# Other orders for the weight sums, the weight forms and the late activation forms of a two-layer transformer's feed-forward blocks

## The chip, the cores and the metric

The kernel runs on one NeuronCore of a Trainium2 chip. The core has a matrix engine (TensorE, PE in the profile, with its weight loads listed apart as PEld), a vector engine (VectorE, DVE), an activation engine (ScalarE, ACT), a general engine (GpSimd, POOL) and a queue engine (SyncE, SP) that issues transfers. The metric is the device time of one execution in microseconds; of several runs the median is taken. Lower is better.

## The reference

A sequence of 512 rows of width 1024 goes through two layers. Each layer has an attention part, which the change does not touch, and a feed-forward part with a squared ReLU:

```python
for l in range(DEPTH):
    ...
    x = x + jnp.einsum('bse,ed->bsd', mixed, w_o[l])

    h = rmsnorm(x, mlp_norm[l])
    u = jnp.square(jax.nn.relu(jnp.einsum('bsd,df->bsf', h, w_ff1[l])))
    x = x + jnp.einsum('bsf,fd->bsd', u, w_ff2[l])
return rmsnorm(x, final_norm)
```

`w_ff1` is 1024 by 4096 and `w_ff2` is 4096 by 1024, both float32.

## The kernel before

**Precision.** Every float32 operand of a product is split into two parts: `hi`, a rounded copy made by ACT (line 114 for weights, 236 or 241 for activations), and `lo`, the rest, made by DVE (line 130, 237 or 242). Three matmuls then stand for one product (`three`, lines 296 to 298). So each block of weights ("unit") costs one ACT instruction `whi` and one DVE instruction `wlo` over 128x1024 elements before PE can use it. Four pairs of buffers hold split weights in the feed-forward part; a unit is split when the unit four places before it has left PE, three units ahead of its use.

**Seven products for eight.** The feed-forward width is cut into 4 groups. In each group both products are done as a 2x2 block product with seven block multiplications in place of eight (Strassen's scheme in Winograd's form). The seven forms are named by their weight operand: `11`, `21` and `22` are quadrants as they lie in memory, `x1` to `x4` are sums of quadrants. The weight sums chain: `x3` = 12 + 22, `x2` = 11 + x3, `x1` = 12 + 11, `x4` = 21 + x2, up to signs. `FORMS` (line 41) is the order in which the seven are multiplied.

**The first product** (`quad_group`, from line 1006; groups 1 to 3, two halves j = 0 and 1 each; units `("s", l, g, j, form)`). Five places in SBUF hold its raw weights, called by letters: a, b, c are buffers of their own (`first_a`, `first_b`, `first_c` in the trace), d is `waves` and e is `norms`. A place serves the forms in `serves` (line 869). `bring` loads a place from memory; e takes two transfers, a load from SP's queue and then an accumulating transfer from POOL's queue that adds the second quadrant, the second waiting for the first. `add` (line 887) sums one place into another on DVE, 128x1024 elements. When each of these is traced is fixed by `then(unit, fn, ...)`: it is traced right after the split of that unit (lines 902 to 914). Results lie in PSUM banks X, V and Y; after form `x1` DVE reads X (line 1036), and form `22` writes into X again, with form `x4` between them in V.

**The second product** (loop from line 1184; units `("f", l, g, form, c)`, c = 0 and 1, 12 matmuls over 512 columns each). Its raw weights live in three kept places, `HOME` (line 43). The sums are made by accumulating transfers in POOL's queue (`grow`, line 857): after the split of `11` its place gets 12 added and becomes `x1`; after `x3` its place gets 11 and becomes `x2`; after `x2` it gets 21 and becomes `x4`; after `21` the place is loaded with 22. Products of `11`, `x2`, `x1` and `22` accumulate on the same two PSUM banks X (`CHAIN`, line 44), `x3` (and in the last group `x4`) on V, `21` on Y, `x4` of the other groups on fresh banks W. After a form whose sum belongs to an output quadrant (`SUMS`, line 45) `gather` (line 1071) reads the two banks into `y`, on DVE (line 1079) or, for a quadrant's first contribution in layer 0, on ACT (line 1077). A form that goes on in X must wait until these reads are done.

**The activation's forms.** The activations of the second product have seven forms too, `sides[j]`. Four are made inside `quad_group`; three late ones (operands for `x2`, `21`, `22`) are made by `rest_of_forms` (line 1053) for both j, the first after both halves and the others after the forms `11`, `x3` and `x2` of the second product.

**What sets the order on an engine.** The program is traced in the order of the code, and a scheduler then orders the instructions of each engine: what was traced first goes first among those that it takes to be ready. Each engine's order is fixed before the run; on the chip every engine works through its queue in that order, and an instruction that waits holds up all behind it on its engine.

Of the kernel before, what the change touches and what calls it, by code (L numbers as in the profile page):

```python
# [13 lines left out]
ALU = mybir.AluOpType  # L14
# [24 lines left out]
DLY_R, DLY_D, DLY_S, DLY_Q = 3.5, 10.2, 9.0, 6.0  # L39
TAIL, ATT, DENSE, CAP = 6.0, 53.0, 145.0, 0.1  # L40
FORMS = ("11", "x3", "x2", "21", "x1", "x4", "22")
SIDE = {"11": 0, "x4": 1, "21": 2, "x1": 3, "x3": 4, "x2": 5, "22": 6}
HOME = {"11": 0, "x1": 0, "x3": 1, "x2": 1, "x4": 1, "22": 2, "21": 2}
CHAIN = {"11": "X", "x2": "X", "x1": "X", "22": "X", "x3": "V", "x4": "V", "21": "Y"}
# [5 lines left out]
def _unit_list():  # L50
    units = []
    def qk(l, cq, ck, b):
        units.append(("p", l, cq + b * P))
        units.append(("p", l, ck + b * P))

    for l in range(L):
        for item in ORDER:
            b = int(item[1])
            if item[0] == "d":
                units.append(("x", l, b, 0))  # L60
                units.append(("x", l, b, 1))
            elif item[0] == "s":
                qk(l, SBQ, SBK, b)
            else:
                for half in range(2):
                    units.append(("v", l, (SBV if item[0] == "u" else DFV) + b * P, half))
        for half in (1, 0):
            for j in range(4):
                units.append(("o", l, half, j))
        for g in range(GROUPS):  # L70
            if g == 0:
                units.extend(("1", l, f) for f in range(2 * GP))
            else:
                units.extend(("s", l, g, j, form) for j in range(2) for form in FORMS)
            for form in FORMS:
                for c in range(GP // 2):
                    units.append(("f", l, g, form, c))
    return units
# [84 lines left out]
def trunk(ctx, tc, opened, xT, w, w2, w1, gfin, lamv, cos, sin, out):  # L163
# [76 lines left out]
    def split_less(hi, lo, src):  # L240
        a = nc.scalar.activation(hi, src, AF.Copy, scale=-1.0)
        nc.vector.scalar_tensor_tensor(
            out=lo, in0=src, scalar=-1.0, in1=hi.bitcast(F32), op0=ALU.mult, op1=ALU.subtract)
        return a
# [87 lines left out]
    for l in range(L):  # L332
        with ExitStack() as actx:
# [476 lines left out]
            for cost in dense(pts if l else None):  # L810
# [5 lines left out]
                while live and credit > 0:  # L816
                    c = next(at, None)
# [17 lines left out]
        with ExitStack() as fctx:  # L835
# [28 lines left out]
            def then(unit, fn, *args):  # L864
                W.then.setdefault(_INDEX[unit], []).append(lambda: fn(*args))

            groups = [(g, j) for g in range(1, GROUPS) for j in range(2)]
            spots = {"d": kept[(2, 1)], "e": norms.rearrange("p a t -> p (a t)")}
            serves = {"a": ("11", "x2"), "b": ("x1",), "c": ("22",), "d": ("21", "x4"), "e": ("x3",)}

            def bring(n, role):
                if n == len(groups):
# [27 lines left out]
                then(("1", l, k), bring, 0, role)  # L900
            then(("f", l, 0, "x2", 1), bring, 0, "e")
            for n, (g, j) in enumerate(groups):
                then(("s", l, g, j, "11"), add, "b", "a")
                then(("s", l, g, j, "x3"), add, "a", "e")
                then(("s", l, g, j, "x3"), bring, n + 1, "e")
                then(("s", l, g, j, "21"), add, "d", "a")
                then(("s", l, g, j, "21"), bring, n + 1, "a")
                then(("s", l, g, j, "x1"), bring, n + 1, "b")
                then(("s", l, g, j, "22"), bring, n + 1, "c")
                if j == 0:  # L910
                    then(("f", l, g - 1, "22", 1), bring, n, "d")
                    then(("s", l, g, j, "x4"), bring, n + 1, "d")
                else:
                    then(("s", l, g, j, "x4"), fetch, g, "21", 1)
# [88 lines left out]
            def chunk(j, k):  # L1003
                return x[:, ((4, 5, 6, 7), (4, 5, 0, 1))[j][k], :]

            def quad_group(g, j, banks_):
# [8 lines left out]
                for form in FORMS:  # L1015
# [9 lines left out]
                    if form == "11":  # L1025
                        nc.scalar.copy(Y, X)
                    elif form == "x3":
                        nc.scalar.copy(v3, V)
                    elif form == "x2":
                        nc.scalar.copy(sx, X)  # L1030
                    elif form == "21":
                        nc.scalar.activation(F[1], Y, AF.Relu)
                        nc.scalar.activation(F[1], F[1], AF.Square)
                        split(hi[0], lo[0], F[1])
                    elif form == "x1":
                        nc.vector.scalar_tensor_tensor(  # L1036
                            out=F[2], in0=X, scalar=-1.0, in1=v3, op0=ALU.mult, op1=ALU.subtract)
                    elif form == "x4":
                        tt2(F[0], V, sx, ALU.add)
                        nc.scalar.activation(both, both, AF.Relu)  # L1040
                        nc.scalar.activation(both, both, AF.Square)
                        split(hi[1], lo[1], F[2])
                        tt2(F[1], F[1], F[0], ALU.subtract)
                        tt2(F[0], F[2], F[0], ALU.subtract)
                        tt2(F[2], F[2], F[1], ALU.add)
                        split(sides[j][0][:, 3:5, :, :].rearrange("p k a t -> p (k a t)"),
                              sides[j][1][:, 3:5, :, :].rearrange("p k a t -> p (k a t)"),
                              x[:, 4:6, :].rearrange("p c t -> p (c t)"))
                    else:
                        nc.scalar.activation(F[3], X, AF.Relu, scale=-1.0)  # L1050
                        nc.scalar.activation(F[3], F[3], AF.Square)

            def rest_of_forms(form):
                for j in range(2):
                    F = [chunk(j, k) for k in range(4)]
                    hi, lo = ([e[:, k, :, :].rearrange("p a t -> p (a t)") for k in range(7)] for e in sides[j])
                    if form == "":
                        split_less(hi[5], lo[5], F[2])
                    elif form == "11":
                        split(hi[2], lo[2], F[3])  # L1060
                    elif form == "x3":
                        tt2(F[3], F[2], F[3], ALU.subtract)
                    elif form == "x2":
                        split(hi[6], lo[6], F[3])

            fresh = set() if last else set(y)

# [95 lines left out]
            for g in range(GROUPS):  # L1163
                end = g == GROUPS - 1
                turn[0] = 0
                if g:
                    p_, q_, r_, s_ = r_, s_, p_, q_
                    quad_group(g, 0, (p_, q_, r_))
                    quad_group(g, 1, (s_, r_, q_))
                    rest_of_forms("")  # L1170
                else:
                    for k in range(2 * GP):
                        for n, pt in enumerate(block(f"f{l}_{g}_{k}", "any")):
# [7 lines left out]
                    p_, q_, r_, s_ = ring[0] % 3, 3, (ring[0] + 1) % 3, (ring[0] + 2) % 3  # L1181
                    held_on = {"Y": [bank("t", f"Y{l}{r}") for r in range(2)], "V": [bank("mm", f"V{l}{r}") for r in range(2)]}
                chains = {"X": [temp(k, f"X{l}{g}{k}") for k in (p_, q_)], **held_on}
                for form in FORMS:
                    total, to = SUMS[form], chains[CHAIN[form]]
                    opens = form == "11" or g == 0 and form in ("x3", "21")
                    if form == "x4" and not end:
# [42 lines left out]
                        break  # L1230
                    if end or form not in ("x3", "21"):
                        came = gather(total, to)
                    if g:
                        rest_of_forms(form)
                    if end and not last and form in ("x2", "21"):
                        for c in range(4 * (form == "21"), 4 * (form == "21") + 4):
                            nc.sync.dma_start(x[:, c, :], park[c])
                    if end and last and form == "x3":
                        for c in range(2):
# [105 lines left out]
```

## Time and profile before

| | |
|---|---|
| median of 3 runs | 1138.74 us (1137.9 to 1139.2) |
| the profiled execution | 1137.62 us |
| its span, first to last instruction | 1135.8 us |
| PE busy | 1120.2 us (99%) |
| DVE busy | 897.8 us (79%) |
| ACT busy | 686.8 us (60%) |
| POOL busy | 151.5 us (13%) |
| HBM read | 152.86 MB |

The profiled execution's own time is 1.8 us above its span, which is what lies around the program's instructions. The page's busy share of PE counts each matmul from its start to its modelled end; since matmuls overlap, the distance between starts tells more. In the timeline each row is one run of equal instructions: start, duration, engine, line, what it writes and reads, and in brackets the idle time of the engine before it and what ended it. In the rows of transfers the last number is the median time from issue to landing.

### The profile page before, as it was taken

The page shows a single profiled execution, that of the slowest core. Times are in us where ns is not written, and L with a number is a line of the kernel's source. Part 1 is how long each engine was busy: PE and PEld are TensorE (multiplying, and loading weights), DVE is VectorE, ACT ScalarE, POOL GpSimd, SP SyncE. Part 2 cuts the span into 40 slices and gives each one's busy share as a digit, 9 for nine tenths or more (in the row PEclk, how much of TensorE's full clock was granted, in tenths as well). Part 3 has the DMA queues.
Part 4 walks back from the last instruction along what each step waited for, and adds up shares of the span by engine and source line. Part 5 has one row for each costly group of instructions (what it writes and reads, how often), then busy time and mean ns, then how long its engine had stood idle before and what let it go on. Part 6 is the DMA issues. An engine that isn't in the chain of part 4 may idle for free.

```text
span 1135.8 us, 17692 instructions
## 1 busy us (share of the span) xinstructions
PE 1120.2 (99%) x6613; PEld 992.8 (87%) x6613; DVE 897.8 (79%) x1313; ACT 686.8 (60%) x1115; POOL 151.5 (13%) x237
## 2 busy tenths in 40 slices
PE   9999999999999999999999999999999999999997
PEld 7899889888889899898888998988888998988975
DVE  7897788789559778787888877887876787786876
ACT  6456666577558457466455565765773574764754
POOL 1000333101101101001000013330011010010010
PEclk9999999999999999999999999999999999999999
DMA  7665353266976857838327644522489679588282
GB/s 263 146 177 148 100 166 108 75 218 166 252 188 167 209 172 168 239 113 214 122 75 197 174 117 142 150 74 75 151 204 231 174 167 235 141 183 223 91 163 79
DMA packets 61621, 183.38 MB, mean 161 GB/s; under 512 B 7520, under 2 KB 8800, under 8 KB 61536
## 3 DMA queue, kind: packets, MB, share of 16 engines
q1 hardware_dynamic: 50160, 141.84, 39.4%
q0 software_dynamic: 10944, 39.85, 20.1%
q8 instruction: 52, 0.85, 0.3%
q10 hardware_dynamic: 432, 0.56, 0.1%
q14 instruction: 33, 0.27, 0.1%
HBM read 152.86 MB, written 4.19 MB: 138 GB/s over the span
## 4 chain that ended last, share of the span: by engine, by line
PE 82%; issue 8%; DMA 4%; DVE 3%; ACT 1%; POOL 1%; POOLq 0%; DVEq 0%; ACTq 0%
PE X L296 6%; PE X L297 6%; PE X L298 6%; PE wo L296 3%; PE wo L297 3%; PE wo L298 3%; PE f L298 3%; PE f L296 3%; PE f L297 3%; PE V L298 2%; PE V L297 2%; PE V L296 2%; DVE wlo L130 2%; PE Y L298 2%; PE Y L297 2%
## 5 line engine op out<-in xcount | busy, mean ns | idle before, releaser
L130 DVE TENSOR_TENSOR wlo<-q,whi 128x1024 fp32r<-128x1024 f32 x96 | 116.7, 1222 | 56.7 <-ACT whi L114 53.6
L114 ACT ACTIVATE whi<-q 128x1024 fp32r<-128x1024 f32 x96 | 100.8, 1056 | 91.7 <-DMA q<-in_w 28.0
L114 ACT ACTIVATE whi<-raw 128x1024 fp32r<-128x1024 f32 (+1 forms) x82 | 80.8, 993 | 50.4 <-issue 20.4
L130 DVE TENSOR_TENSOR wlo<-raw,whi 128x1024 fp32r<-128x1024 f32 (+1 forms) x82 | 95.2, 1168 | 12.1 <-ACT whi L114 11.6
L296 PE MATMUL X<-whi,Ah 128*128 128x512 f32 x248 | 97.8, 395 | 1.9 <-ACT whi L114 1.3
L297 PE MATMUL X<-wlo,Ah 128*128 128x512 f32 x248 | 97.4, 393 | 0.8 <-DVE wlo L130 0.8
L298 PE MATMUL X<-whi,Al 128*128 128x512 f32 x248 | 97.1, 391 | 0.0
L862 POOL DMA_DIRECT2D q<-in_w x48 | 42.4, 884 | 237.3 <-DVE wlo L130 223.9
L130 DVE TENSOR_TENSOR wlo<-waves,whi 128x1024 fp32r<-128x1024 f32 x40 | 48.9, 1222 | 17.1 <-ACT whi L114 17.1
L114 ACT ACTIVATE whi<-waves 128x1024 fp32r<-128x1024 f32 x40 | 42.3, 1057 | 32.7 <-PE X L298 16.6
L296 PE MATMUL X<-hxh,whi 128*128 128x256 f32 x192 | 54.6, 285 | 3.4 <-DVE x L1036 3.4
L296 PEld LDWEIGHTS X<-whi,Ah 128*128 128x128 f32 x248 | 46.9, 189 | 12.2 <-ACT whi L114 1.7
L297 PEld LDWEIGHTS X<-wlo,Ah 128*128 128x128 f32 x248 | 47.0, 190 | 10.4 <-DVE wlo L130 1.1
L298 PEld LDWEIGHTS X<-whi,Al 128*128 128x128 f32 x248 | 47.0, 189 | 9.9
L298 PE MATMUL X<-h_hi,wlo 128*128 128x256 f32 x192 | 54.3, 283 | 0.0
L297 PE MATMUL X<-h_lo,whi 128*128 128x256 f32 x192 | 54.3, 283 | 0.0
L298 PE MATMUL X<-hxh,wlo 128*128 128x256 f32 x192 | 54.3, 283 | 0.0
L297 PE MATMUL X<-hxl,whi 128*128 128x256 f32 x192 | 54.3, 283 | 0.0
L296 PE MATMUL X<-h_hi,whi 128*128 128x256 f32 x192 | 54.3, 283 | 0.0
L236 ACT ACTIVATE Ah<-x 128x512 fp32r<-128x512 f32 (+1 forms) x60 | 42.6, 710 | 16.5 <-DVE x L940 16.1
L296 PE MATMUL f<-h_hi,whi 128*128 128x512 f32 x128 | 50.3, 393 | 0.0
L298 PE MATMUL f<-h_hi,wlo 128*128 128x512 f32 x128 | 49.9, 390 | 0.0
(738 smaller groups left out, 3805.3 us busy)
## 6 DMA issues: line engine op xcount, KB each, us to landing
raw<-in_w SPq DMA_DIRECT2D x78, 512.0 KB, 3.7
q<-in_w POOLq DMA_DIRECT2D x64, 512.0 KB, 6.6
q<-in_w SPq DMA_DIRECT2D x48, 512.0 KB, 5.4
waves<-in_w SPq DMA_DIRECT2D x28, 512.0 KB, 5.5
first_a<-in_w SPq DMA_DIRECT2D x12, 512.0 KB, 3.8
first_b<-in_w SPq DMA_DIRECT2D x12, 512.0 KB, 4.8
first_c<-in_w SPq DMA_DIRECT2D x12, 512.0 KB, 3.5
norms<-in_w SPq DMA_DIRECT2D x12, 512.0 KB, 3.7
```

Of the source, the lines that this page charges most:

```text
L114: return self.nc.scalar.activation(o, src, AF.Copy)
L130: self.last = h, nc.vector.tensor_tensor(out=lo[:, a:b], in0=raw[:, a:b], in1=hi[:, a:b].bitcast(F32), op=ALU.subtract)
L236: a = nc.scalar.activation(hi, src, AF.Copy)
L296: nc.tensor.matmul(pt, ah, bh, start=first, stop=False, skip_group_check=goes_on)
L297: nc.tensor.matmul(pt, ah, bl, start=False, stop=False, skip_group_check=goes_on)
L298: nc.tensor.matmul(pt, al, bh, start=False, stop=last, skip_group_check=goes_on)
L862: nc.gpsimd.dma_start(t, quad(g, q, c), accum_op=ALU.add)
```

## The change

It has three parts.

1. **First product.** The place e now serves `x3` and `x2`, and a serves `11` alone: after the split of `x3`, a is added into e (before, e was added into a). The sum b += a is traced after the split of `21` in place of after that of `11`. The sum into d is taken from e. The next load of e is traced after the split of `21`, behind that of a, in place of after that of `x3`. The number of sums (3) and of transfers is the same.
2. **Second product.** A second order, `FORMS2`, is used for it: `21` comes third and `x2` fourth. So `x2` and `x1`, both on X, now stand side by side, and `x2` stands four units behind `x3` in place of two.
3. **Late activation forms.** `rest_of_forms` takes one j. For j = 0 the three are traced inside the second half of `quad_group` (after `11`, `x3`, `x2`), for j = 1 after both halves and after `11` and `x3` of the second product. The operand of `21` comes first, then that of `x2`, then that of `22`.

```diff
 FORMS = ("11", "x3", "x2", "21", "x1", "x4", "22")
+FORMS2 = ("11", "x3", "21", "x2", "x1", "x4", "22")
...
-            for form in FORMS:
+            for form in FORMS2:
                 for c in range(GP // 2):
                     units.append(("f", l, g, form, c))
...
-            serves = {"a": ("11", "x2"), "b": ("x1",), "c": ("22",), "d": ("21", "x4"), "e": ("x3",)}
+            serves = {"a": ("11",), "b": ("x1",), "c": ("22",), "d": ("21", "x4"), "e": ("x3", "x2")}
...
             for n, (g, j) in enumerate(groups):
-                then(("s", l, g, j, "11"), add, "b", "a")
-                then(("s", l, g, j, "x3"), add, "a", "e")
-                then(("s", l, g, j, "x3"), bring, n + 1, "e")
-                then(("s", l, g, j, "21"), add, "d", "a")
+                then(("s", l, g, j, "x3"), add, "e", "a")
+                then(("s", l, g, j, "21"), add, "b", "a")
+                then(("s", l, g, j, "21"), add, "d", "e")
                 then(("s", l, g, j, "21"), bring, n + 1, "a")
+                then(("s", l, g, j, "21"), bring, n + 1, "e")
                 then(("s", l, g, j, "x1"), bring, n + 1, "b")
                 then(("s", l, g, j, "22"), bring, n + 1, "c")
...
                     else:
                         nc.scalar.activation(F[3], X, AF.Relu, scale=-1.0)
                         nc.scalar.activation(F[3], F[3], AF.Square)
-
-            def rest_of_forms(form):
-                for j in range(2):
-                    F = [chunk(j, k) for k in range(4)]
-                    hi, lo = ([e[:, k, :, :].rearrange("p a t -> p (a t)") for k in range(7)] for e in sides[j])
-                    if form == "":
-                        split_less(hi[5], lo[5], F[2])
-                    elif form == "11":
-                        split(hi[2], lo[2], F[3])
-                    elif form == "x3":
-                        tt2(F[3], F[2], F[3], ALU.subtract)
-                    elif form == "x2":
-                        split(hi[6], lo[6], F[3])
+                    if j and form in ("11", "x3", "x2"):
+                        rest_of_forms(0, {"11": "21", "x3": "x2", "x2": "22"}[form])
+
+            def rest_of_forms(j, form):
+                F = [chunk(j, k) for k in range(4)]
+                hi, lo = ([e[:, k, :, :].rearrange("p a t -> p (a t)") for k in range(7)] for e in sides[j])
+                if form == "21":
+                    split(hi[2], lo[2], F[3])
+                elif form == "x2":
+                    split_less(hi[5], lo[5], F[2])
+                elif form == "22":
+                    tt2(F[3], F[2], F[3], ALU.subtract)
+                    split(hi[6], lo[6], F[3])
...
-                    rest_of_forms("")
+                    rest_of_forms(1, "21")
...
-                for form in FORMS:
+                for form in FORMS2:
...
-                    if g:
-                        rest_of_forms(form)
-                    if end and not last and form in ("x2", "21"):
-                        for c in range(4 * (form == "21"), 4 * (form == "21") + 4):
+                    if g and form in ("11", "x3"):
+                        rest_of_forms(1, "x2" if form == "11" else "22")
+                    if end and not last and form in ("21", "x2"):
+                        for c in range(4 * (form == "x2"), 4 * (form == "x2") + 4):
                             nc.sync.dma_start(x[:, c, :], park[c])
```

## The prediction

> **What bounds the kernel now.** I read the page first, then the waits of PE, then all waits, then timelines around each place where PE stood still.
>
> ```profile
> PE 1120.2 (99%) x6613; PEld 992.8 (87%) x6613; DVE 897.8 (79%) x1313; ACT 686.8 (60%) x1115; POOL 151.5 (13%) x237
> PE X L296 <- DVE x L1036: 3.4, 3, 2.4
> PE X L296 <- ACT whi L114: 1.3, 1, 1.3
> PE X L297 <- DVE wlo L130: 0.8, 1, 0.8
> PE X L296 <- DVE y L1079: 0.6, 1, 0.6
> ```
>
> PE is the bound, and its matmuls stay as they are. The rows of waits (total, times, longest) show all that PE loses in the feed-forward parts: 3.4 + 1.3 + 0.8 + 0.6 = 6.1 us in six stops. The change can gain these and what follows each, and no more; it can lose without such a limit.
>
> The 3.4 us: DVE reads X after form `x1` (line 1036), and `22` waits for that.
>
> ```profile
> 336.19 1.23 DVE L888 TENSOR_TENSOR first_b<-first_b,first_a 128x1024 f32<-128x1024 f32 x1 [5.62 <-DMA first_b<-in_w]
> 341.47 0.68 DVE L1036 SCALAR_TENSOR_TENSOR x<-X,x 128x512 f32<-128x512 f32 x1
> 339.41 0.28 PE L297 MATMUL V<-h_lo,whi 128*128 128x256 f32 x1
> 339.53 0.28 PE L298 MATMUL V<-h_hi,wlo 128*128 128x256 f32 x1
> 342.20 0.39 PE L296 MATMUL X<-hxh,whi 128*128 128x256 f32 x1 [2.40 <-DVE x L1036]
> DVE first_b L888 <- DMA first_b<-in_w: 20.7, 6, 5.6
> ```
>
> DVE stood 5.62 us at the sum b += a, whose b had not landed; everything behind it came late, line 1036 among it, and PE stopped 2.40 us. Six such stops of DVE make 20.7 us; three reached PE.
>
> The 1.3 and 0.8 us lie in the last group of layer 1, at `x2` of the second product:
>
> ```profile
> 1086.47 0.63 ACT L1243 ACTIVATE x<-x 128x512 f32<-128x512 f32 x1 [2.72 <-DMA x<-in_gfin]
> 1098.94 1.06 ACT L114 ACTIVATE whi<-q 128x1024 fp32r<-128x1024 f32 x1 [3.65 <-DMA q<-in_w]
> 1095.84 0.40 PE L296 MATMUL X<-whi,Ah 128*128 128x512 f32 x1
> 1100.05 0.51 PE L296 MATMUL X<-whi,Ah 128*128 128x512 f32 x1 [1.32 <-ACT whi L114]
> 1101.89 0.62 PE L296 MATMUL X<-whi,Ah 128*128 128x512 f32 x1
> 1102.31 0.63 PE L297 MATMUL X<-wlo,Ah 128*128 128x512 f32 x1
> 1105.53 0.39 PE L296 MATMUL Y<-whi,Ah 128*128 128x512 f32 x1
> 1101.90:1105.30 3.40, 3.40 (x10) 2.63 (x9) 3.40 (x5) 1.03 (x2) 0.59 (x1) 0.50 0.71 123
> ```
>
> ACT waited for the accumulated weights of the second `x2` unit. The form lasted from 1095.84 to 1105.53, 9.69 us, also because the clock was halved after the two stops: in the last row (a stretch, the busy time of PE, PEld, DVE, ACT and POOL in it, then granted clock, DMA share and GB/s) it is 0.50 over 3.40 us, and matmuls start 0.42 apart.
>
> The 0.6 us is `x2` waiting for DVE's reading of X after `11`, in the last group of layer 0.
>
> ```profile
> 532.86 0.39 PE L298 MATMUL V<-whi,Al 128*128 128x512 f32 x1
> 533.80 0.47 PE L296 MATMUL X<-whi,Ah 128*128 128x512 f32 x1 [0.56 <-DVE y L1079]
> 387.12 0.39 PE L296 MATMUL X<-whi,Ah 128*128 128x512 f32 x1
> 392.56 0.39 PE L296 MATMUL W<-whi,Ah 128*128 128x512 f32 x1
> ```
>
> **The change part by part.** An undisturbed form of the second product takes 392.56 - 387.12 = 5.44 us, a unit 2.72, one of its 24 matmuls 0.23.
>
> *`x2` fourth, gain.* Its weights are accumulated after the split of `x3`, now four units ahead in place of two: 2 x 2.72 = 5.44 us more. The disturbed form lost 9.69 - 5.44 = 4.25 us. With `whi` at 1098.94 as before and PE reaching that unit 5.44 us later, it is in time: I take the whole 4.25. The wait for gfin at 1086.47 is not touched; that it may eat into this is a rival. The stop at 533.80 goes too, since two forms now lie between `11` and `x2`: starts 0.94 us apart in place of 0.23, gain 0.7.
>
> *b += a later, gain.* The sum is traced two splits later. Yet the scheduler takes sums from far ahead: the row below, in the middle of group 1's second half, is the sum for group 2.
>
> ```profile
> 357.99 1.22 DVE L888 TENSOR_TENSOR first_b<-first_b,first_a 128x1024 f32<-128x1024 f32 x1
> 353.19 0.69 DVE L242 SCALAR_TENSOR_TENSOR Al<-x,Ah 128x512 fp32r<-128x512 f32 x1
> 342.50:365.30 22.80, 22.80 (x192) 22.80 (x192) 20.92 (x24) 18.13 (x24) 2.70 (x4) 1.00 0.63 161
> ```
>
> The sum needs only a and b, so it can still be put where DVE seems free and b has not landed on the chip. Ends: 0 and 3.4 us; I take half, 1.7.
>
> *The late forms, nothing.* They are the same instructions. The row at 353.19 is line 242, the late form of `x2` for j = 0, run in the second half although traced after it: what part 3 asks for is done already. The cover is DVE's room there, 20.92 of 22.80 us busy; without it each of the four DVE steps would cost 0.69.
>
> *`x2` next to `x1`, loss.* `x1` writes the banks that the gather of `x2` reads, eight times. What the wait would be shows at today's `x1`:
>
> ```profile
> 391.14 1.23 DVE L130 TENSOR_TENSOR wlo<-q,whi 128x1024 fp32r<-128x1024 f32 x1 [1.49 <-ACT whi L114]
> 392.28 1.40 DVE L1079 SCALAR_TENSOR_TENSOR y<-X,r,y 128x512 f32<-128x512 f32 x2
> 381.68 0.39 PE L296 MATMUL Y<-whi,Ah 128*128 128x512 f32 x1
> 382.48 1.41 DVE L1079 SCALAR_TENSOR_TENSOR y<-X,r,y 128x512 f32<-128x512 f32 x2
> 573.21 0.48 PE L436 MATMUL p1w<-mdh,h_hi 128*128 128x256 f32 x2
> 573.80 0.73 PE L296 MATMUL p<-h_hi,whi 128*128 128x512 f32 x2
> ```
>
> The two readings take 1.40 us, 0.7 each, and start behind the `wlo` of a unit to come. The first ends at 392.98, 0.42 after the form's end at 392.56; with the signal about 0.5 us of PE. The second bank is then free when its turn comes, three matmuls (0.7 us) later. That gives 8 x 0.5 = 4.0 us. Queued behind the stopped `x1` on PE are `x4`'s matmuls, on other banks; the rows at 573 show the scheduler putting matmuls of a later block (p1w) among earlier ones (p) that were not ready. If it does so here, two `x4` matmuls (0.46 us) fill each gap. Ends 0 and 4.0; I take 2.0.
>
> *e freed later, loss.* e now holds `x2` as well and is free only after d += e. DVE's sums and the queues around group 1's first half:
>
> ```profile
> 325.51 1.22 DVE L888 TENSOR_TENSOR waves<-waves,first_a 128x1024 f32<-128x1024 f32 x1
> 320.35 0.33 SPq L881 DMA_DIRECT2D norms<-in_w  x1
> 326.80 0.33 SPq L881 DMA_DIRECT2D first_a<-in_w  x1
> 327.19 0.87 POOL L883 DMA_DIRECT2D norms<-in_w  x1 [10.81 <-DMA norms<-in_w]
> norms<-in_w SPq DMA_DIRECT2D x1, 512.0 KB, 6.2
> norms<-in_w POOLq DMA_DIRECT2D x1, 512.0 KB, 8.7
> norms<-in_w SPq DMA_DIRECT2D x12, 512.0 KB, 3.7
> norms<-in_w POOLq DMA_DIRECT2D x12, 512.0 KB, 5.8
> ```
>
> SP's load moves from 320.35 to about 328.0 (325.51 plus two sums of 1.22), behind that of a; b and d queue behind it as they do now. POOL's adding transfer stands behind the load, 0.6 us after its landing (320.35 + 6.2 to 327.19). With this place's landings e is whole at 328.0 + 6.2 + 0.6 + 8.7 = 343.5; with the medians of the twelve at 328.0 + 3.7 + 0.6 + 5.8 = 338.1. It is needed for `x3` of the second half. Without the 2.40 stop `22` starts at 339.65, and two forms of 2.88 (24 matmuls of 0.12, as from 339.41 to 339.53) later `x3` at 345.41; before it come `whi` (1.06) and `wlo` (1.22), so e must be there by 343.1. Then `x2` follows only after the sum e += a: 1.06 + 1.22 + 1.22 + 1.06 + 1.22 = 5.8 us from landing, due 348.29. On medians this hides; on the slow landings it is 343.5 + 5.8 - 348.29 = 1.0 us late, 1.7 with one more DVE step of 0.69 ahead, and six halves (3 groups, 2 layers) have this turn. The other way round (second half to next group) a whole second product lies between, which hides it. Ends 0 and 6 x 1.7 = 10.2; nearer the medians, I take 1.0.
>
> **Sum:** -4.25 - 0.7 - 1.7 + 2.0 + 1.0 = -3.65 us. The profiled execution's 1137.62 (span 1135.8 and 1.8 around it) becomes 1133.97; it lies 1.12 below the median of the runs, so the forecast for the median is 1138.74 - 3.65 = **1135.1 us**.
>
> **The rivals.**
>
> *All gains, no losses.* The gaps at `x1` are filled, e lands on medians, b += a moves behind the landing: 1138.74 - 4.25 - 0.7 - 3.4 = 1130.4. For it: the rows at 573 and the medians. Against: the row at 357.99.
>
> *The change doesn't do what it says.* The scheduler puts b += a where it was, the gfin wait keeps half of the last group's loss: -0.7 - 2.1 + 3.0 = +0.2, so 1138.9.
>
> *e comes too late: slower.* The e chain above at the slow landings in most of the six halves. It decides from 3.65 + 1.0 = 4.65 us in all, 0.8 per half; at its full price of 10.2 the time is 1135.1 + 9.2 = 1144.3. For it: the two serial transfers, and DVE's 20.92 of 22.80 us in the second half. Against: this place's landings are the slow ones.
>
> *The gather of `x2` runs late on DVE.* At today's `x2` the pair of readings began at 382.48 behind a late `wlo`; the first ended 1.5 us after that form's end (381.68, where `21` starts). Eight of these unfilled are 12.0 us: 1145.1. Against: there `wlo` was late because `x2` came early; in fourth place it should look as at 391.14.
>
> *The clock falls.* After each stop at `x1` the clock could fall to 0.50 as at 1101.90: eight matmuls of 0.42 in place of 0.23, 1.5 us, eight times 12: 1147.1. Against: the stop of 2.40 us at 342.20 was followed by clock 1.00 over 342.5 to 365.3. [...]
>
> **How the numbers follow.** Forecast 0.36; all gains 0.20; doesn't do it 0.13; e too late 0.20; gather late 0.09; clock 0.02. A measurement of this kernel tells about 0.2% (2.3 us) from no change. Faster: 0.33 of the forecast, all of the second, 0.03 of the third, 0.56. Within: 0.03, 0.07 of the third, 0.03 of the fourth, 0.13. Slower: 0.03, 0.17, 0.09, 0.02, 0.31. The range goes from a little under the best case, 1129.5, to 1142.5, which takes in the milder half of the late e; left out are its dearer half and the last two. The forecast's own range is 1132 to 1137.
>
> **What would show it.** Right: no stop of PE at `x2` in the last group and no half clock there; the longest wait of DVE for `first_b` under 2 us and line 1036 gone from PE's waits; `X` waiting for `y` L1079 with eight stops of at most 0.5 us, or `W` matmuls among those of `X`; `whi<-norms` of the second halves hardly waiting. Wrong: ACT waiting several us for `norms`, with PE stops at `wlo` in the second halves; `first_b` stops as long as now; new stops in layer 0's first group, where `21` now stands third.

## The result, and the profile after

| | before | after |
|---|---|---|
| median of the runs compared | 1139.2 us (1137.9 to 1140.35, 5 runs) | 1158.83 us (1156.34 to 1161.41, 5 runs) |
| the profiled execution | 1137.62 us, span 1135.8 | 1161.41 us, span 1159.6 |

The changed kernel is slower: ratio 1.0172, 95% interval 1.0154 to 1.0191, some 20 us. The rows of PE's waits after the change (total, times, longest, in us; all line numbers are one higher than before):

```profile
PE X L297 <- ACT Y L1027: 9.6, 6, 2.6
PE W L297 <- ACT whi L115: 7.1, 1, 7.1
PE V L298 <- DVE wlo L131: 2.4, 2, 1.3
PE X L297 <- DVE y L1080: 0.5, 3, 0.2
PE X L297 <- DVE x L1037: 0.5, 2, 0.2
```

The stops of before are nearly gone from X: DVE's reading of X fell from 3.4 to 0.5 us, `whi` and `wlo` no longer stop X in the last group. Two new rows are each larger than all that was saved, and a third, the stops at V (2.4 us), is new too. The first consists of six stops of one kind, the second is one stop.

**The six stops** stand in the second halves (j = 1) of the first product: form `x2` may not write X before ACT has copied X, the result of `11`, to Y (line 1027). Two of the six, each as ACT's wait before it splits e (`norms`) for `x3` and PE's stop some 11 us later, and what ACT did in between in the first of them (the timeline of after; the bracket is the idle time before the row and its end):

```profile
350.67 1.06 ACT L115 ACTIVATE whi<-norms 128x1024 fp32r<-128x1024 f32 x1 [1.98 <-DMA norms<-in_w]
354.34 1.06 ACT L115 ACTIVATE whi<-norms 128x1024 fp32r<-128x1024 f32 x1 [2.61 <-DVE norms L889]
359.90 1.04 ACT L115 ACTIVATE whi<-waves 128x1024 fp32r<-128x1024 f32 x1
360.84 0.58 ACT L1027 COPY Y<-X 128x512 f32<-128x512 f32 x1
361.47 0.39 PE L297 MATMUL X<-hxh,whi 128*128 128x256 f32 x1 [1.22 <-ACT Y L1027]
...
920.10 1.06 ACT L115 ACTIVATE whi<-norms 128x1024 fp32r<-128x1024 f32 x1 [3.34 <-DMA norms<-in_w]
930.89 0.38 PE L297 MATMUL X<-hxh,whi 128*128 128x256 f32 x1 [2.58 <-ACT Y L1027]
```

In each of the six pairs PE's stop is ACT's wait less 0.75 to 0.77 us (1.98 and 1.22, 1.79 and 1.02, 2.29 and 1.52, 3.34 and 2.58, 1.41 and 0.66, 3.30 and 2.54). Only the wait of 1.41 us is put down to DVE's reading of X (line 1037), which ended at 1001.10; e landed at the same time, 7.3 us after its addition was issued at 993.76. In the first pair ACT has no pause between 354.34 and the copy at 360.84, so by as much as it waits for e it is late with the copy; in all six only some 0.76 us of that is slack.

**The one stop** lies in the first group of layer 0, at the new neighbourhood of `x2` and `x1`. POOL's, ACT's and PE's rows there, then the stretch behind it (clock, DMA share and GB/s are the last three numbers):

```profile
302.35 0.87 POOL L884 DMA_DIRECT2D norms<-in_w  x1 [13.29 <-PE Y L299]
302.91 2.12 POOL L863 DMA_DIRECT2D q<-in_w  x2
313.58 1.06 ACT L115 ACTIVATE whi<-q 128x1024 fp32r<-128x1024 f32 x1 [10.36 <-DMA q<-in_w]
314.55 1.25 ACT L1078 ACTIVATE y<-X,r 128x512 f32<-128x512 f32 x2
314.69 0.79 PE L297 MATMUL W<-whi,Ah 128*128 128x512 f32 x1 [7.13 <-ACT whi L115]
315.28 0.78 PE L297 MATMUL X<-whi,Ah 128*128 128x512 f32 x1
314.70:318.10 3.40, 3.40 (x8) 2.56 (x9) 2.21 (x2) 2.15 (x3) 0.00 (x0) 0.50 0.48 95
318.10:322.00 3.90, 3.90 (x13) 3.08 (x12) 0.33 (x2) 1.06 (x1) 0.88 (x1) 0.64 0.79 223
```

```profile
293.90 0.86 POOL L862 DMA_DIRECT2D q<-in_w  x1 [6.15 <-DVE wlo L130]
296.96 0.88 POOL L862 DMA_DIRECT2D q<-in_w  x1 [2.19 <-DVE wlo L130]
301.58 0.88 POOL L883 DMA_DIRECT2D norms<-in_w  x1 [3.75 <-DMA norms<-in_w]
```

The second fence is the timeline of before. There the two growths of `x4` (`q`) were issued at 293.90 and 296.96, one after the other and ahead of the addition into e. With `x2` one form later they come at 302.91, both at once and behind that addition. ACT's `whi` for `x4` waits 10.36 us for the first of them. Behind it in ACT's queue stands the gather of `x2`, which in this group is ACT's (line 1078), since the quadrant has no contribution yet. `x1` needs the banks that it reads. PE stood 7.13 us, took one `x4` matmul (W) at 314.69 and then `x1` at 315.28. The clock stood at 0.50 for 3.4 us and at 0.64 for 3.9 us more: 3.4 x 0.50 + 3.9 x 0.36 = 3.1 us lost besides. So 9.6 + 7.1 + 3.1 = 19.8 us lie in two places.

**The whole account.** The two profiled executions have spans 23.8 us apart, more than the medians, since the one after is the slowest of its five and the one before lies 1.6 us under its median. Divided at the start of the first matmul of each stretch, the spans compare so (us):

| stretch | before | after | difference |
|---|---|---|---|
| all ahead of layer 0's feed-forward part | 284.30 | 285.61 | +1.31 |
| first group of layer 0 | 38.08 | 48.57 | +10.49 |
| the six first products | 246.05 | 255.93 | +9.88 |
| the other second products, without the last group of each layer | 190.59 | 193.18 | +2.59 |
| last second product of layer 0 and the attention part of layer 1 | 325.53 | 325.04 | -0.49 |
| last second product of layer 1, to the end | 51.25 | 51.27 | +0.02 |

The 9.88 us hold the six stops, the lower clock behind one of them (0.65 over 3.4 us from 930.90, 1.2 us) and, with the other sign, the 2.9 us less at DVE's reading of X; some 2 us of them are not placed. Nor are the 1.31 us, in a part that the change does not touch. The last row shows that nothing of the gain forecast for the last group was left at the end.

### The profile page after: what moved, and what is told of

The parts are those of the page before. It is cut to its first block, busy times and chain, and to the rows that moved or that the text cites. A ratio compares the mean times of both kernels' runs of the same rounds, so it can differ in the third digit from the quotient of the medians.

```text
span 1159.6 us, 17684 instructions
## 1 busy us (share of the span) xinstructions
PE 1128.6 (97%) x6613; PEld 994.7 (86%) x6613; DVE 899.8 (78%) x1313; ACT 685.9 (59%) x1115; POOL 151.8 (13%) x237
## 4 chain that ended last, share of the span: by engine, by line
PE 63%; DMA 12%; issue 9%; DVE 7%; ACT 5%; POOL 2%; SPq 0%; POOLq 0%; ACTq 0%; DVEq 0%
DMA q<-in_w 7%; PE X L297 4%; DMA norms<-in_w 4%; PE X L298 4%; PE X L299 4%; DVE wlo L131 3%; PE wo L297 3%; PE wo L298 3%; PE wo L299 3%; ACT whi L115 2%; PE f L299 2%; PE f L297 2%; PE f L298 2%; DVE y L1080 1%; PE V L298 1%
## 5 line engine op out<-in xcount | busy, mean ns | idle before, releaser
L297 PE MATMUL X<-whi,Ah 128*128 128x512 f32 x248 | 99.1, 399 | 0.5 <-DVE y L1080 0.5
L297 PE MATMUL X<-hxh,whi 128*128 128x256 f32 x192 | 55.9, 291 | 10.1 <-ACT Y L1027 9.6
L115 ACT ACTIVATE whi<-norms 128x1024 fp32r<-128x1024 f32 x24 | 25.4, 1060 | 56.9 <-DVE norms L889 32.9
L297 PEld LDWEIGHTS X<-whi,Ah 128*128 128x128 f32 x248 | 47.3, 191 | 13.2 <-DVE y L1080 2.9
L115 ACT ACTIVATE whi<-waves 128x1024 fp32r<-128x1024 f32 x40 | 42.2, 1054 | 23.8 <-PE X L299 12.3
L297 PE MATMUL X<-h_hi,whi 128*128 128x256 f32 x192 | 54.3, 283 | 0.0
L297 PE MATMUL f<-h_hi,whi 128*128 128x512 f32 x128 | 50.3, 393 | 0.0
L238 DVE TENSOR_TENSOR Al<-x,Ah 128x512 fp32r<-128x512 f32 (+1 forms) x60 | 47.1, 792 | 4.1 <-ACT Ah L237 4.1
```

The source lines that it names most:

```text
L115: return self.nc.scalar.activation(o, src, AF.Copy)
L238: nc.vector.tensor_tensor(out=lo, in0=src, in1=hi.bitcast(F32), op=ALU.subtract)
L297: nc.tensor.matmul(pt, ah, bh, start=first, stop=False, skip_group_check=goes_on)
```

## The experiments

All of them, with the median of each, its range, the kernel before on the same chip, and the ratio of the two:

| | runs | before | ratio, 95% |
|---|---|---|---|
| p1_only | 1156.36 (1150.37 to 1159.94) | 1139.04 | 1.0150 [1.0105, 1.0194] |
| p2_only | 1145.77 (1144.48 to 1148.77) | 1139.04 | 1.0073 [1.0048, 1.0099] |
| p3_only | 1139.28 (1134.99 to 1140.87) | 1139.04 | 1.0003 [0.9983, 1.0024] |
| p23 | 1146.57 (1145.33 to 1149.47) | 1139.04 | 1.0073 [1.0049, 1.0098] |
| a_first_e | 1155.18 (1154.72 to 1155.73) | 1138.53 | 1.0139 [1.0117, 1.0160] |
| a_x4_behind | 1159.38 (1158.61 to 1163.81) | 1138.53 | 1.0185 [1.0151, 1.0219] |
| a_e_single | 1137.45 (1134.23 to 1139.46) | 1138.53 | 0.9985 [0.9969, 1.0000] |
| b_e_late | 1138.64 (1135.18 to 1142.76) | 1138.53 | 1.0002 [0.9982, 1.0022] |
| a_gather | 1150.25 (1148.39 to 1153.30) | 1139.01 | 1.0104 [1.0079, 1.0130] |
| a_gather_e | 1145.83 (1143.52 to 1148.56) | 1139.01 | 1.0060 [1.0039, 1.0082] |
| best3 | 1140.78 (1135.81 to 1143.80) | 1139.01 | 1.0008 [0.9988, 1.0027] |
| best4 | 1133.04 (1132.26 to 1133.45) | 1139.01 | 0.9950 [0.9932, 0.9968] |
| a_copy | 1143.49 (1142.78 to 1147.66) | 1136.80 | 1.0070 [1.0044, 1.0096] |
| b_badd | 1139.75 (1135.62 to 1142.66) | 1136.80 | 1.0027 [1.0011, 1.0042] |
| a_all | 1161.98 (1159.08 to 1162.52) | 1138.08 | 1.0197 [1.0173, 1.0221] |

**The parts one by one.** Each kernel is the one before with one hunk of the diff, or the changed one without part 1.

p1_only: the changes to `serves` and `then` alone.

> Part 1 (weight sums and loads of the first product) alone on the kernel before. Theory E (e is free only after the sum into d, so its two serial transfers end late; ACT stands at the split of x3 and its copy of X into Y comes late, six times): 1143 to 1148 us, with PE waits on ACT Y of 8 to 11 us in the six second halves, less some 3 us of waits on DVE x that go. Rival P (the loss comes from the order of the second product): 1136 to 1140, no PE waits on ACT Y.

p2_only: `FORMS2` alone, and in `rest_of_forms` the operand of `22` behind `21`:

```diff
-                    elif form == "x2":
+                    elif form == "21":
                         split(hi[6], lo[6], F[3])
```

> Part 2 (21 before x2 in the second product) alone on the kernel before; the operand of 22 is made after 21 in place of after x2. Theory W (matmuls of x4 are put ahead of x1 on PE, and in layer 0's first group the growth of x4's weights queues on POOL behind the load of e, whose place in the code moves with x2): 1142 to 1150, with one PE wait of 5 us or more on ACT whi of W in layer 0's first group. Rival (part 1 makes all the loss): 1132 to 1138.

p3_only: the late forms by half alone. The operand of `x2` stays first, since `x2` is third here.

> Part 3 (late activation forms by half) alone on the kernel before; the operand of x2 stays first, since x2 is third. Theory: the scheduler runs them where it did; 1138 to 1140.5. Rival (DVE overfilled in the second halves): 1142 or more, PE waits on DVE x or wlo in second halves.

p23: parts 2 and 3.

> The changed kernel with part 1 undone (parts 2 and 3 kept). Theory E says it is 8 to 11 us below the changed kernel but with the 3 us of waits on DVE x back: 1148 to 1154 and no PE waits on ACT Y. If part 1 made nothing of the loss: 1157 to 1160.

Part 3, so ordered, does nothing that can be measured. Part 1 alone costs 17.3 us, part 2 alone 6.7, and parts 2 and 3 together 7.5, so part 1 adds only about 12 to that. The parts interact, as PE's waits of part 1 alone show:

```profile
PE X L296 <- DVE y L1079: 8.0, 5, 2.0
PE X L296 <- ACT Y L1026: 7.0, 6, 1.8
```

With `x2` still third, the gather of `11` stops it five times too (8.0 us); two forms between them, as part 2 has it, hide that. This profiled execution took 1150.37 us and is the fastest of its four, so the 15.0 us of these two rows stand for it and not for the median, 6 us higher. The row of `Y` belongs to part 1, the 7.5 us at `W` (p2_only's `PE W L297`) to part 2.

**The stop of 7.1 us.** Four kernels, each the changed one with an edit.

a_first_e traces the first load of e one form later:

```diff
-            then(("f", l, 0, "x2", 1), bring, 0, "e")
+            then(("f", l, 0, "21", 1), bring, 0, "e")
```

> The changed kernel with one edit: the first load of e in each layer is traced after the second unit of 21 (third form), as before by place, in place of after x2 (now fourth). Theory W: POOL's adding transfer for e then stands ahead of the growth of x4's weights no longer, the stop of 7.1 us at W in layer 0's first group goes with the half clock behind it, 8 to 11 us less: 1148 to 1151. Rival (x4's growth is slow by itself): 1157 to 1160 with the stop still there.

A miss: the stop stayed at 6.9 us. That POOL still issued the addition into e ahead of the growths is the author's estimate, from the changed kernel's 302.35 and 302.91; no row of this run shows it. The 3.7 us that came off, on another chip, are not explained by it.

a_x4_behind keeps every `x4` matmul behind the last of `x1`:

```diff
+                        if form == "x1":
+                            x1_last = m[2]
+                        elif form == "x4":
+                            behind(m[0], x1_last)
```

> The changed kernel with one edit: an order edge keeps every matmul of x4 behind the last of x1. PE then waits for the reading of X after x2 (0.3 to 0.6 us, eight times) in place of taking a matmul of x4 early. Theory W: x1's 5.4 us are done while the late weights of x4 land, so the stop of 7.1 us falls to some 2; 1150 to 1156 in all. Rival (the reading of X is the cost, my forecast's term): 1160 or more, with 3 to 5 us of waits on DVE y.

```profile
PE X L297 <- ACT y L1078: 7.1, 1, 7.1
PE X L297 <- DVE y L1080: 5.7, 7, 2.2
968.80:972.20 3.40, 3.40 (x15) 2.83 (x16) 1.74 (x2) 0.98 (x2) 0.00 (x0) 1.00 0.71 214
```

The stop is the same, now plainly at the gather on ACT, so the `x4` matmul that PE had taken ahead is not its cause. Of the other seven `x2`-`x1` neighbours five cost what one row of before had said, 0.44 to 0.50 us; the others are 1.04 us in layer 0's second group and 2.25 us in the last group of layer 1. The last row is the stretch behind one stop of 0.49 us, at a clock of 1.00, as behind all seven.

a_gather puts the gather of `x2` ahead of the split of `x4`'s first unit, on ACT or DVE:

```diff
+                        whole = total in fresh
                         came = gather(total, to)
+                        if form == "x2":
+                            of = W.head_of if whole else W.rest_of
+                            behind(of[_INDEX[("f", l, g, "x4", 0)]], came[1])
```

> The changed kernel with one more rule of order: behind each x2 of the second product, the gather goes ahead of whi (on ACT) or wlo (on DVE) of x4's first unit. Theory: the 7.1 us stop in layer 0's first group is the gather standing in ACT's queue behind a whi that waits 10.4 us for its accumulated weights. With the gather ahead, x1 runs while those weights land, and what is left is a stop at x4 of 1 to 3 us; the matmuls at half clock behind the long stop (3.4 us) go too: 1158.8 - 5 - 3.4 = 1150.4, range 1148.5 to 1153.5. The six ACT Y stops of the first product (9.6 us in all) stay. Rival: the late weights themselves set the time, and the stop only moves from x1 to x4, with the half clock behind it: 1156 to 1159.

```profile
312.95 0.50 PE L299 MATMUL W<-whi,Ah 128*128 128x512 f32 x1 [0.84 <-ACT whi L116]
314.21 0.50 PE L300 MATMUL W<-wlo,Ah 128*128 128x512 f32 x1 [0.76 <-DVE wlo L132]
314.20:317.60 3.40, 3.39 (x15) 2.78 (x16) 2.12 (x2) 3.22 (x5) 0.00 (x0) 1.00 0.53 158
```

As the theory said: `x1` runs while the growth lands, 0.84 + 0.76 us are left at `x4`, and the clock behind them is 1.00. The median is 8.6 us lower, on another chip; the ratio to before fell from 1.0172 to 1.0104.

a_gather_e adds the first load of e behind `x1`'s first unit, and its addition on POOL behind `x4`'s second growth:

```diff
+                        if n == 0:
+                            behind(d, grown[("x4", 1)])
...
-            then(("f", l, 0, "x2", 1), bring, 0, "e")
+            then(("f", l, 0, "x1", 0), bring, 0, "e")
```

> As the one before, and e's first load is traced behind x1 of the first group, its accumulating transfer issued behind x4's second growth on POOL, as it stood before the change. Theory: x4's growths then wait for one transfer fewer, and no PE stop over 1 us is left in layer 0's first group: about 10.6 us below the changed kernel, 1148.2, range 1146.5 to 1150.5; the e loss of the six halves (about 10 us) stays alone. Rival: the growths are slow by themselves, and the order on POOL gives nothing beyond the gather's: the same as the gather's rule alone within 1 us.

4.4 us less again, and no stop of PE in that group; this is more than the 1.6 us left there, and part of it is the `Y` stops of that profile (8.8 in place of 12.1 us), which vary. Growth order and ACT order together make up part 2's loss.

**The place e.** a_e_single is the changed kernel whose e holds quadrant 12 alone; the addition of quadrant 22 is left out, with its transfer.

```diff
-                quads = {... "e": ("12", "22")}[role]
+                quads = {... "e": ("12",)}[role]
```

> The changed kernel, where e gets quadrant 12 alone (the adding transfer of 22 is left out, so the output differs). Theory E: e is whole 7 to 10 us earlier, ACT no longer stands at its split, the 9.6 us of PE waits on ACT Y go, and layer 0's POOL queue is free for x4's growth, so the stop at W goes too: 1136 to 1142. Rival (the longer chain split, sum, split of e is what delays ACT's copy): waits on ACT Y stay above 4 us, 1146 or more.

```profile
PE W L297 <- ACT whi L115: 0.7, 1, 0.7
```

The six stops at `Y` are gone, and nine tenths of the stop at `W`; the two growths of `x4`, with no addition ahead of them, are issued at 299.21 and 300.41, in place of 302.91. What is left at V, 1.5 us, lies in the last group. Without this transfer the rest of the change saves 0.15% (interval 0 to 0.31%).

b_e_late is the kernel before with e's load traced where the change has it, e serving `x3` alone as before:

```diff
-                then(("s", l, g, j, "x3"), bring, n + 1, "e")
...
+                then(("s", l, g, j, "21"), bring, n + 1, "e")
```

> The kernel before with one edit: the next load of e is traced after the split of 21, as in the changed kernel, while e still serves x3 alone. If what delays e is that it is in use until the sum into d, the scheduler still issues the load as soon as a += e is done: 1137 to 1141, no PE waits on ACT Y. If the place in the code delays it: 1144 or more with PE waits on ACT Y.

No difference, and the transfer did not move: e's load is issued at 320.63 and 343.40 (320.35 and 343.31 before). So the place in the code does not set the time of the load. In the changed kernel e is in use until d += e, and there it goes out at 338.61.

a_copy is a_gather_e with ACT's copy of X to Y ahead of `whi` of `21` in the second halves:

```diff
+                        kept_x = nc.scalar.copy(Y, X)
+                        if j:
+                            behind(W.head_of[_INDEX[("s", l, g, j, "21")]], kept_x)
```

> The changed kernel with the gather's and the first e's order as above, and one more: in each second half (j = 1) whi of 21 goes behind ACT's copy of X to Y, so that the copy comes one ACT instruction (1.04 us) earlier. Theory: PE does not wait for late weights of x2, it waits for ACT's in-order queue, in which the copy stands behind whatever ACT did late after waiting for e. Then each of the six gaps at x2 (1.27, 2.03, 2.49, 1.19, 0.94, 0.93; 8.8 us) shrinks by up to 1.04, 5.9 us in all, and about 2.9 us of X <- ACT Y are left: 1145.8 - 5.9 = 1139.9, range 1138.5 to 1142. Rival: e itself is late by as much, so the stop only moves to whi or wlo of x2 or 21: 1144.5 to 1147, with new rows of PE waiting for whi or wlo.

```profile
PE X L299 <- DVE x L1045: 4.3, 4, 1.5
PE X L299 <- ACT x L1039: 1.4, 3, 0.5
PE X L299 <- ACT Y L1033: 1.1, 3, 0.4
ACT whi L116 <- DMA norms<-in_w: 10.4, 6, 2.1
339.75 1.06 ACT L116 ACTIVATE whi<-norms 128x1024 fp32r<-128x1024 f32 x1 [1.71 <-DMA norms<-in_w]
```

The stops at `Y` fell from 8.8 to 1.1 us, and PE did not come to wait for `whi` or `wlo` of `x2` or `21`: the weights were in time, the copy was not. The ratio to before did not follow (1.0070, against 1.0060 without the edit on another chip; the intervals overlap): 3.7 us more (4.3 for 0.6) and 1.4 us came back at the next readers of PSUM, DVE's reading of X (line 1045 here) and ACT's next copy (line 1039). Neither theory had that.

a_all adds to it b += a behind `wlo` of the unit it is traced after:

```diff
+                if to == "b":
+                    behind(made, W.last[1])
```

> The kernel before this one (the changed kernel with the gather's, the first e's and the copy's order) with b += a on DVE behind wlo of the unit that it is traced after. Theory: with the copy earlier, form 22 of the second half runs into DVE's reading of X, which stands behind the early b += a (359.27 to 360.49, then wlo and Al, the reading at 362.15); without that sum ahead the four stops at X <- DVE x (4.3 us) go: a ratio to before of about 1.007 - 0.004 = 1.003, range 0.999 to 1.005. Rival: DVE is full there whatever the order, and the stops move to another reader or wlo: 1.006 to 1.009.

```profile
PE X L299 <- ACT Y L1035: 15.6, 6, 3.5
ACT whi L116 <- DMA norms<-in_w: 30.0, 6, 5.7
327.64 0.33 SPq L886 DMA_DIRECT2D first_a<-in_w  x1
328.78 0.33 SPq L886 DMA_DIRECT2D norms<-in_w  x1
342.40 1.06 ACT L116 ACTIVATE whi<-norms 128x1024 fp32r<-128x1024 f32 x1 [4.54 <-DMA norms<-in_w]
```

A miss by some 20 us, and telling. The row at DVE's reading of X is down from 4.3 to 0.7 us. But a is in use until that sum and is reloaded later, at 327.64 and 1.1 us ahead of e; in a_copy it goes 6.0 us ahead of it:

```profile
321.92 0.33 SPq L886 DMA_DIRECT2D first_a<-in_w  x1
327.94 0.33 SPq L886 DMA_DIRECT2D norms<-in_w  x1
```

e's load goes out 0.8 us later than there and its addition 1.3 us later, which then takes 8.8 us in place of 7.4. So e comes 2.65 us later at this place (342.40 for 339.75), ACT waits 30.0 us in place of 10.4, and the stops at `Y` grow to 15.6. The arrival of e sets the loss, through ACT.

**A version that beats both.** best3 is p2_only with the two orders of a_gather_e; best4 is best3 with the order of b += a shown above; b_badd is the kernel before with that last order alone.

> The kernel before with part 2 alone (21 third, x2 fourth in the second product), with both orders: the gather of x2 ahead of the split of x4's first unit, and e's first accumulating transfer behind x4's second growth. Theory: part 2 alone cost 7.0 us net, of which the stop of 7.5 us at W <- whi in the first group and the half clock behind it (3.4 us) are all of the loss; without them its gain is left, 4 to 5 us in the last group less 0.1 to 0.5 at each x1: 1145.8 - 10 = 1135.8, range 1133 to 1138. Rival: x2 next to x1 costs on average as forecast (2 to 4 us) and the last group's gain was eaten by later waits: 1138 to 1141.

> The one before, with the sum b += a ordered on DVE behind the wlo of the unit that it is traced after, which the scheduler otherwise takes early. Theory: DVE then stands no more than 1 us for first_b, the stops of PE at X <- DVE x (3.4 us in the kernel before, 2.1 with part 2 alone) go, and 1 to 3 us come off: 1132 to 1136. Rival: the sum moves its 1.22 us of DVE into a place where the wlo of the next unit stands behind it, and the gain is given back there: the same as the one before within 0.5 us, or slower with stops at wlo.

> The kernel before with one rule of order alone: b += a on DVE goes behind wlo of the unit that it is traced after. Theory: the scheduler's early place for this sum costs the stops of PE at X <- DVE x (3.4 us in the profiled run, and what makes its runs scatter from 1136 to 1143.8); without it the runs lie within 2 us of each other at 1139.0 - 3.4 = 1135.6, range 1134 to 1137, and best4's further 2 to 3 us are part 2's gain in the last group. Rival 1: all of best4's gain is this order: 1132.5 to 1133.5, part 2 is worth nothing. Rival 2: only with part 2 does the order help: 1138 to 1140.

PE's largest wait in the feed-forward parts, first of best3 and then of best4:

```profile
PE X L299 <- DVE x L1043: 4.3, 4, 1.4
```

```profile
PE V L299 <- ACT whi L116: 1.2, 1, 1.2
```

best4 takes 1133.04 us, 0.5% less than before (interval 0.32 to 0.68%), with six runs within 1.2 us of each other where the twenty of before spread over 7.8. In the profiles, 3.85 us of the gain lie in the six first products and 2.25 in the stretches of the two last second products. best3's 1140.78 missed its expectation, although its profiled run took 1136.93: the early b += a is still in it and gives back what part 2 saves. That sum's order alone gives nothing either; b_badd is 0.27% slower. Its timeline in the last group of layer 0:

```profile
532.89 1.41 DVE L1081 SCALAR_TENSOR_TENSOR y<-X,r,y 128x512 f32<-128x512 f32 x2
533.79 0.47 PE L296 MATMUL X<-whi,Ah 128*128 128x512 f32 x1 [1.89 <-DVE y L1081]
```

The gather is at 532.89 as before (PE went on at 533.80 then, after 0.56 us), so PE, come earlier, waits 1.89. What DVE does there waits for ACT's `whi` of accumulated weights and comes no earlier (`wlo` at 531.15 after 4.57 us idle, before at 531.16 after 3.76), so time won ahead of it is lost there. By the same stretches b_badd's profile has 3.7 us less than before in the six first products and 3.4 more in three of the second products. The gain needs both: `x2` fourth and the sum in its place. Why b_badd's median is slower rather than equal stays open.

## Why the prediction was wrong, by its own steps

*`x2` fourth, gain:* right in the wait, wrong in the size. X no longer waits in the last groups for weights (1.3 + 0.8 us) or for `y` (0.6). In layer 0 the stretch is 0.49 us shorter, of 0.7 forecast. In layer 1, of 4.25 us, nothing is left. PE, come earlier, stops at the next late weights instead, and both stops at V lie there:

```profile
1118.29 0.50 PE L298 MATMUL V<-wlo,Ah 128*128 128x512 f32 x1 [1.14 <-DVE wlo L131]
1132.71 1.22 DVE L131 TENSOR_TENSOR wlo<-q,whi 128x1024 fp32r<-128x1024 f32 x1
1133.85 1.40 DVE L1080 SCALAR_TENSOR_TENSOR y<-X,r,y 128x512 f32<-128x512 f32 x2
1133.98 0.49 PE L298 MATMUL V<-wlo,Ah 128*128 128x512 f32 x1 [1.26 <-DVE wlo L131]
1134.65 0.50 PE L297 MATMUL X<-whi,Ah 128*128 128x512 f32 x1 [0.17 <-DVE y L1080]
```

The first is in `x3`, which takes 7.12 us from its first matmul to that of the next form, 5.82 before. The second is at `x1`, the last neighbour of `x2`: PE took two `x4` matmuls (V) ahead and stood at the second for `wlo`, and DVE's gather stands behind that same `wlo`. `x1` starts 3.07 us behind the last matmul of `x2` (1131.58); that one and the two taken make 0.68 of it, so 2.4 us are lost. These 1.3 + 2.4 us and 0.5 us from form `22` on are the 4.25.

The step asked only whether the weights of `x2` come in time, and not what PE meets next; and it asked only of the last group what moves with `x2`. The same move brings the growth of `x4` to the addition into e in layer 0's first group.

*b += a later, gain:* PE's row fell by 2.9 us. DVE's row, now `DVE first_b L889 <- DMA first_b<-in_w` with 14.0 us in 9 waits, longest 3.5, shows that the scheduler still takes sums early; the sign set for it, under 2 us, was not reached.

*Late forms, nothing:* right, as far as p3_only shows it.

*`x2` next to `x1`, loss:* right in size at most of the places where DVE gathers: 0.44 to 0.50 us where nothing fills the gap (a_x4_behind), less where `x4` matmuls do. It was too low in the last group of layer 1 (2.4 us, above), and it failed where ACT gathers. The step priced one row of a later group for all eight places; "a quadrant's first contribution in layer 0" is on ACT, and behind a `whi` whose weights are late. 7.1 + 3.1 us, in place of at most 0.5.

*e freed later, loss:* the step that failed most, at **"on medians this hides"**. Its date for the load was good, its landing was not. Form `22` of the first half starts at 351.45 in the profile after, 11.80 us behind the 339.65 of the forecast. So moved, the forecast had e's load at 339.8 and e whole at 349.9 on medians; the load is at 338.61, earlier than that, and ACT starts on e at 350.67, later. The addition is what grew: in the six second halves it took 7.7, 7.5, 7.9, 7.6, 7.3 and 8.1 us, where the forecast took the median of before, 5.8 (those six were 8.7, 5.6, 5.6, 5.7, 6.4 and 5.9 then). What slowed it no run separates; in a_copy the one of the six that took 5.7 us has ACT's shortest wait, 0.85 us. Still, `wlo` of `x2` in this half ends at 355.43 + 1.23 = 356.66, its due time was 348.29 + 11.80 = 360.09: 3.4 us to spare.

```profile
norms<-in_w POOLq DMA_DIRECT2D x12, 512.0 KB, 8.0
355.43 1.23 DVE L131 TENSOR_TENSOR wlo<-norms,whi 128x1024 fp32r<-128x1024 f32 x1 [0.58 <-ACT whi L115]
```

The weights of e did hide. What did not is ACT's wait of 1.4 to 3.3 us for them, with the copy of X to Y queued behind. The trace of before could have told how little room that copy had:

```profile
349.39 0.59 ACT L1026 COPY Y<-X 128x512 f32<-128x512 f32 x1
350.94 0.28 PE L296 MATMUL X<-hxh,whi 128*128 128x256 f32 x1
```

It ended at 349.98, and `x2` started 0.96 us later. The step asked when the waiting instruction's own result is due, not what stands behind it on its engine. This cost 9.6 us in place of 1.0, below its upper end of 10.2, by another way than the one priced. Both errors were needed: with 5.8 us for each of the six additions ACT would have been late by more than the 0.76 us in two of the halves only, and PE's stops would come to some 1.1 us (an estimate from the issue times of after). That is near the 1.0 taken, so the sum of this step hung on the median, which did not hold at the new place.

*The rivals:* "e comes too late" had the cause (landings nearer the slow one than the median, in all six halves), the sign and, at its full price, the size of part 1's share; with `wlo` as the place PE would stop it had the wrong mechanism. "The gather of `x2` runs late on DVE" came true in one place of eight, the last group of layer 1. "The clock falls" was wrong for seven of the eight neighbours (1.00 over the 3.4 us behind each in a_x4_behind) and right for the long stop (0.50). Of the signs listed, ACT's wait for `norms` and new stops in layer 0's first group are what came. The sum with what was measured in three terms: 1.0 and 0.25 us (an eighth of 2.0) out and 9.6 + 7.1 + 3.1 in make -4.9 + 19.8 = +14.9 us, and without the 4.25 of the last group, which did not come, +19.2. Measured were +19.6 on medians and +23.8 between the profiled executions, so the agreement is rough: what the account above does not place stays open.

## What to carry to other kernels

Price a wait at its engine, not at its result: name the next instruction behind it that another engine needs, and read its slack from the trace of before. Here ACT's copy had 0.96 us in the trace of before, the weights 3.4 in that of after. When a stop is to go, ask what the engine, come earlier, will stop at next; here that took back 4.25 us of 4.25. When an order moves, follow each transfer that moves with it to what now shares its queue, in every group, the first above all. Its old landing time did not carry over here: e's addition took 7.3 to 8.1 us at the new place, against a median of 5.8 before. And two edits that each give nothing can give a gain together, when each removes the stop that took the other's gain back: here ratios of 1.0008 (best3) and 1.0027 (b_badd), and 0.9950 together (best4).

## What the hardware showed that was not expected

Clock: the stop of 2.58 us at 930.89 was followed by a clock of 0.65, the one of 2.54 us at 1093.85 by 1.00:

```profile
930.90:934.30 3.40, 3.40 (x20) 3.40 (x21) 3.40 (x4) 3.05 (x5) 0.00 (x0) 0.65 0.00 0
1093.90:1097.30 3.40, 3.40 (x29) 3.40 (x30) 3.40 (x4) 3.04 (x5) 0.00 (x0) 1.00 0.00 0
```

In a_gather a stop of 3.27 us was followed by 1.00 over 3.4 us, and one of 1.94 us by 0.55. So at 2 to 3 us the length of the stop alone did not set the clock in these runs.
